# PEER encoder step on one core: w parts queued one operation later, five V buffers, two scattered tiles and three built ones

## The chip, the core and the metric

The kernel runs on one core of a Trainium2 chip. Its engines run side by side, each through its own instructions in program order: PE (TensorE, matrix products), DVE (VectorE), ACT (ScalarE), POOL (GpSimd, which also issues the indirect DMAs here) and SP (SyncE, which here only issues plain DMAs). An instruction that waits holds up everything behind it on its engine. The metric is the device time of one execution in microseconds (us), lower is better.

## The reference

The model is one layer of a streaming encoder for 1024 prompt frames and 64 sample frames of width 1024. A mixer (window attention and retention) is followed by a normalisation, then comes a feed-forward part with 16384 experts ("PEER"), which is what this change is about:

```python
s1, i1 = lax.top_k(s[:, :, 0], PEER_TOPK)          # 8 heads, 16 of 128 keys, twice
s2, i2 = lax.top_k(s[:, :, 1], PEER_TOPK)
cand_s = s1[..., :, None] + s2[..., None, :]       # 256 candidates per head
cand_i = i1[..., :, None] * N_KEYS + i2[..., None, :]
top_s, sel = lax.top_k(cand_s, PEER_TOPK)          # 16 experts per head, 128 per frame
eidx = jnp.take_along_axis(cand_i, sel, axis=-1)
g = jax.nn.softmax(top_s, axis=-1)
act = jax.nn.gelu(jnp.einsum('tpkd,td->tpk', u_tab[eidx], xb))
w = (g * act).astype(xb.dtype)
return jnp.einsum('tpk,tpkd->td', w, v_tab[eidx])
```

A frame thus has 128 pairs of an expert number and a weight g. Two heads of a frame may choose the same expert, and one head chooses 16 different ones. The output is the weighted sum of the 128 rows of `v_tab`.

## The kernel before

The 1088 frames are eight prompt tiles of 128 frames (0 to 7) and one tile TS of 64 frames. The program has three stages.

**Head.** In four groups of tiles ([TS,0,1], [2,3], [4,5], [6,7]) it computes projection, attention, retention, normalisation and the scores of the keys. A generator `route` per tile finds the 128 experts and weights. It is fed into the engines' queues in small pieces.

The feed-forward part takes two ways. For the tiles TS, 5, 6, 7 the rows of U and V are **gathered**: each of 64 + 3 x 128 = 448 slots is one indirect DMA issued by POOL (`uv`, line 239, 128 rows of 8 KB). Then DVE takes the dot product with the frame (`uv<-uv,ph`), ACT the gelu and the weight (`gav`), and DVE adds the weighted V row to `pacc`. There are four `uv` buffers (`NB`). A gather into a buffer waits for the `pacc` four slots before it.

For the tiles 0 to 4 (`DENSE`) a matrix G with a weight for each of the 16384 experts and each frame is made in HBM, and all experts are computed. G comes about in two ways:
- Tiles in `SCAT` are **scattered**: the tile's G is cleared by eight 1 MB writes of `zeros`. Then 128 indirect DMAs of POOL (line 373, `G<-sg,si`) each add one weight per frame in place. Scatters into the same G follow each other: each waits until the one before it into that G has landed. `scatter()` puts them into the program in the head, in turn over the tiles. All tiles share POOL's one queue.
- Tiles in `MIDT` are **built** in the second stage.

**Mid.** For a tile in `MIDT`, 32 steps make G from one-hot matrices. In a step DVE compares an index with a ramp (`ob`, bf16) for both halves of the expert number. POOL multiplies one by the weight (`oh<-ob,gT`) in three steps of four, and ACT turns the other to float (`oh<-ob`). In the remaining step of four DVE does it alone (`oh<-iota,gT`, four instructions, and `oh<-gT,iota`). PE multiplies them (`pG`), and ACT copies the result to `gs`. Every 16 steps 4 MB of `gs` are written to G. Beside that, mid feeds in the rest of `route` (tiles 6, 7), eight splits of the frames into a high and a low part (`xhi` on ACT, `xlo` on POOL), the first U tiles, and one scatter per step as long as some are left.

**Dense.** 128 blocks of 128 experts go through two operations. `u_mm(i)` on PE: 48 pairs of products of U's high and low parts with the frames into `pA`. Then ACT takes the gelu in place (`pA<-pA`), DVE multiplies with G (`ge<-pA,gt`), ACT makes the high part (`wh<-ge`) and POOL the low part (`wl<-ge,wh`). `v_mm` on PE: products of wh and wl with V's parts (`vh`, `vl`) for three blocks, one tile and half the width into `y`, which DVE adds to `Y`. In a group of three blocks stand three `u` operations, for the next group, and ten `v` operations. Each operation also issues the split of parts needed later: `uh` (ACT) and `ul` (POOL) of U from `ur`, `vh` (ACT) and `vl` (POOL) of V from `vr`. At each `yield` the outer loop may add up to a few gather slots. A cost model in the program, `est`, decides how many.

The order on each engine is that of the program text: whatever `u_mm` issues for ACT and POOL behind its second `yield` stands ahead of the gathers and splits that come after.

Of the kernel before, what the change touches and what calls it, by code (L numbers as in the profile page):

```python
# [9 lines left out]
F32 = mybir.dt.float32  # L10
# [5 lines left out]
OP = mybir.AluOpType  # L16
# [11 lines left out]
EPS = 1e-5  # L28
NEG = -1e30
GROUPS = [[TS, 0, 1], [2, 3], [4, 5], [6, 7]]  # L30
SCAT, MIDT = [0, 1, 2], [3, 4]
DENSE = SCAT + MIDT
ND = len(DENSE) * 128
GW = max(sum(ROWS_S if t == TS else 128 for t in g) for g in GROUPS)
# [6 lines left out]
BK = (5, 5, 5, 5, 5)  # L41
CRATE, CRMAX = 0.92, 7.0
LINK = 2.75
SCC, GTC = 1.55, 1.1
TP = 64
ATS = 4
OHB = (6, 4)
# [88 lines left out]
def hymba_peer_step(ctx, tc, a, o):  # L136
# [224 lines left out]
    def now():  # L361
        return max(est.t["pe"], est.t["dve"])
# [4 lines left out]
    def scatter(rush=0):  # L367
        n = 0
        for t in sorted(SCAT, key=lambda t: links[t]):
            if t in sc and links[t] < 128 and (n < rush or (due[t] <= now() and ctl["pq"] <= now() + 5.0)):  # L370
                g, idx = sc[t]
                j = links[t]
                nc0.gpsimd.indirect_dma_start(  # L373
                    out=spill[t]["G"], out_offset=bass.IndirectOffsetOnAxis(ap=idx[:, j:j + 1], axis=0),
                    in_=g[:, j:j + 1], in_offset=None, compute_op=OP.add)
                est.t["pool"] += 1.0
                ctl["pq"] = max(ctl["pq"], now()) + SCC
                links[t] = j + 1
                due[t] = max(due[t], now() - 3 * LINK) + LINK
                n += 1  # L380
        return n
# [856 lines left out]
    def dense(hx):  # L1238
# [13 lines left out]
        def u_fill(last):  # L1252
            while un[0] < min(last + 1, 128):
                u = up.tile([128, KC, 128], F32, name="ur")
                nc.sync.dma_start(u, a["ut"][un[0]])
                uq[un[0]] = [u]
                un[0] += 1
# [12 lines left out]
        def x_load(k):  # L1270
            xr.append(up.tile([128, ND], F32, name="xr", tag="ur"))
            nc.sync.dma_start(xr[-1], h1T_d[:, k])

        def x_split(k):
            x = xr.pop(0)
            nc.scalar.activation(xhi[:, k], x, AF.Copy)
            nc.gpsimd.tensor_tensor(xlo[:, k], x, xhi[:, k].bitcast(F32), op=OP.subtract)
# [11 lines left out]
        with ExitStack() as mx:  # L1289
            for m, _ in enumerate(mid(mx)):  # L1290
                if m % 4 == 0 and 0 <= m // 4 - 1 < KC + 2:
                    k = m // 4 - 1
                    if k >= 2:
                        x_split(k - 2)
                    if k < KC:
                        x_load(k)
                if m == 48:
                    u_fill(1)
                if m == 54:
                    u_split(0)  # L1300
                if m == 57:
                    u_split(1)
                scatter(1)
        log("mid")
# [10 lines left out]
        vp = hx.enter_context(tc.tile_pool(name="vp", bufs=NVS))  # L1315
# [12 lines left out]
        def vbase(g, h):  # L1328
            return 2 * GO[g] + h * BGS[g]
# [5 lines left out]

        def v_fill(last):
            while vn[0] < min(last + 1, NV):
                v = vp.tile([128, 512], F32, name="vr", bufs=4)
                nc.sync.dma_start(v, a["vt"][vseq[vn[0]]])
                vq[vn[0]] = [v]  # L1340
                vn[0] += 1
# [10 lines left out]
        def u_mm(i):  # L1352
            uh, ul = uq.pop(i)
            G = gq[i // 2][:, :, i % 2]
            if i % 2:
                gq.pop(i // 2)
            p = pA.tile([128, 2, 512], F32, name="pA")
            n = 0
            for l, x in ((uh, xhi), (uh, xlo), (ul, xhi)):
                for k in range(KC):  # L1360
                    for f in range(2):
                        nc.tensor.matmul(p[:, f, 0:NF], l[:, k], x[:, k, f * NF:(f + 1) * NF], start=n == 0,
                                         stop=n == 3 * KC - 1)
                    n += 1
            u_upto(i + 2)
            if i < BGS[0]:
                v_upto(i + 1)
            yield
            nc.scalar.activation(p[:, :, 0:NF], p[:, :, 0:NF], AF.Gelu_apprx_tanh)
            ge = up.tile([128, ND], F32, name="ge")  # L1370
            nc.vector.tensor_tensor(ge.rearrange("p (f n t) -> p f n t", f=2, t=TP),
                                    p[:, :, 0:NF].rearrange("p f (n t) -> p f n t", t=TP),
                                    G.rearrange("p (f n) t -> p f n t", f=2), op=OP.mult)
            whi = wp.tile([128, ND], F32R, name="wh")
            wlo = wp.tile([128, ND], F32R, name="wl")
            nc.scalar.activation(whi, ge, AF.Copy)
            nc.gpsimd.tensor_tensor(wlo, ge, whi.bitcast(F32), op=OP.subtract)
            wq[i] = (whi, wlo)
# [4 lines left out]
        def v_mm(g, h, t):  # L1383
# [11 lines left out]
            else:  # L1395
                v_upto(vbase(g, 1) + 1 + zs.index((h, t)))
            yield
            dst = Y[:, t, h * 512:(h + 1) * 512]
            if g == 0:
                nc.vector.scalar_tensor_tensor(dst, dst, ALPHA, p, op0=OP.mult, op1=OP.add)  # L1400
# [22 lines left out]
        for g in range(NG):  # L1423
            v = [("v", (g, h, t)) for h in range(2) for t in range(NT)]
# [171 lines left out]
```

## Time and profile before

| | |
|---|---|
| time, median of 3 runs | 3572.55 us (3553.33 to 3574.36) |
| profiled execution: its time, its span | 3574.14 us, 3572.4 us |
| busy in the span: PE, DVE, POOL, ACT | 81%, 64%, 55%, 30% |
| head | 0 to about 1022 us |
| mid | about 1022 to 1362 us |
| dense | 1362 us to the end |

The stage bounds are read from the instructions: the first `ob` of mid starts at 1022.44 us, the last `gs` ends at 1362.1 us. Busy time is the time in which an engine executes something. An engine can be busy half of the time and still be the one that all others wait for, if what it does stands in the wrong order. So beside the busy time the waits are read: for every engine, what ended its idle time.

### The profile page before, as it was taken

How to read it: one execution, taken by the hardware profiler on the slowest of the kernel's cores; microseconds unless marked ns; L12 is line 12 of the kernel's file. 1: busy time of each engine (PE TensorE's matmuls, PEld its weight loads, DVE VectorE, ACT ScalarE, POOL GpSimd, SP SyncE). 2: the span in 40 equal slices, each digit the busy share in tenths (PEclk: the TensorE clock that was granted, in tenths of full speed). 3: DMA queues.
4: the chain of work that ended last, by engine and by line, in shares of the span. 5: the costliest groups of instructions: out<-in, count | busy, mean ns of one | idle time of the engine just before them, and what ended most of it. 6: DMA issues, size and time to landing. Idle time of an engine off the chain costs nothing.

```text
span 3572.4 us, 43054 instructions
## 1 busy us (share of the span) xinstructions
PE 2882.9 (81%) x14953; PEld 2472.0 (69%) x14953; DVE 2273.7 (64%) x5456; ACT 1069.5 (30%) x2542; POOL 1966.4 (55%) x1430
## 2 busy tenths in 40 slices
PE   5999888998930555988888888888888888888896
PEld 3776676776720445877777777777777777778785
DVE  1438849667340992477777777777777767767734
ACT  2322332423300452232323232333233323322322
POOL 0000365665676986566565665566656655656544
PEclk8999999998965667999999999999999999999998
DMA  6337435454421356588888888888889988888841
GB/s 191 113 108 259 137 85 137 109 130 92 87 27 0 62 115 186 172 326 337 310 328 315 339 317 332 338 322 321 329 343 344 344 310 331 321 314 324 341 140 65
DMA packets 305762, 812.82 MB, mean 228 GB/s; under 512 B 80264, under 2 KB 169720, under 8 KB 238472
## 3 DMA queue, kind: packets, MB, share of 16 engines
q0 software_dynamic: 119808, 470.01, 38.4%
q1 hardware_dynamic: 185304, 339.73, 27.7%
q8 instruction: 118, 1.93, 0.2%
q14 instruction: 100, 0.82, 0.1%
q10 hardware_dynamic: 432, 0.33, 0.0%
HBM read 752.84 MB, written 56.84 MB: 227 GB/s over the span
## 4 chain that ended last, share of the span: by engine, by line
DMA 14%; issue 14%; PE 13%; POOL 11%; DVE 7%; ACT 2%; SPq 0%; POOLq 0%; DVEq 0%; ACTq 0%
DMA uv<-uv,gi 12%; PE y L108 7%; PE pA L108 6%; DVE pacc L108 4%; POOL uv L239 4%; POOL vl L108 4%; POOL ul L108 1%; POOL wl L108 1%; DVE uv L108 1%; DVE Y L108 1%; DVE ge L108 1%; ACT wh L108 1%; DMA gt<-G 1%; DMA ur<-ut 1%; POOL Y L108 0%
## 5 line engine op out<-in xcount | busy, mean ns | idle before, releaser
L373 POOL DMA_INDIRECT G<-sg,si x384 | 607.7, 1583 | 696.7 <-DMA G<-zeros 382.6
L108 DVE SCALAR_TENSOR_TENSOR uv<-uv,ph 128x1024 f32<-128x1024 f32 x448 | 544.2, 1215 | 296.8 <-DMA uv<-uv,gi 288.4
L108 PE MATMUL y<-vh,wh 128*128 128x512 f32 x1280 | 534.1, 417 | 241.2 <-DVE Y L108 223.5
L108 DVE SCALAR_TENSOR_TENSOR pacc<-uv,gav,pacc 128x1024 f32<-128x1024 f32 x448 | 575.4, 1284 | 24.0 <-ACT gav L108 21.0
L239 POOL DMA_INDIRECT uv<-uv,gi x448 | 432.3, 965 | 286.6 <-DVE pacc L108 213.6
L108 PE MATMUL y<-vl,wh 128*128 128x512 f32 x1280 | 525.8, 411 | 19.0 <-POOL vl L108 19.0
L108 PE MATMUL y<-vh,wl 128*128 128x512 f32 x1280 | 523.9, 409 | 0.0
L108 POOL TENSOR_TENSOR wl<-ge,wh 128x640 fp32r<-128x640 f32 x128 | 200.3, 1565 | 562.2 <-ACT wh L108 507.0
L108 PEld LDWEIGHTS y<-vh,wh 128*128 128x128 f32 x1280 | 253.3, 198 | 327.8 <-DVE Y L108 207.8
L108 DVE TENSOR_TENSOR Y<-y,Y 128x512 f32<-128x512 f32 x420 | 280.4, 684 | 179.9 <-PE y L108 174.8
L108 PE MATMUL pA<-xhi,uh 128*128 128x320 f32 x2048 | 337.9, 319 | 33.7 <-DVE ge L108 33.7
L108 PEld LDWEIGHTS pA<-xhi,uh 128*128 128x128 f32 x2048 | 330.6, 199 | 47.5 <-DVE ge L108 34.5
L108 POOL TENSOR_TENSOR vl<-vr,vh 128x512 fp32r<-128x512 f32 x256 | 326.1, 1292 | 11.6 <-ACT vh L108 8.7
L108 PE MATMUL pA<-xhi,ul 128*128 128x320 f32 x2048 | 321.2, 309 | 0.0
L108 PE MATMUL pA<-xlo,uh 128*128 128x320 f32 x2048 | 321.2, 309 | 0.0
L108 POOL TENSOR_TENSOR ul<-ur,uh 128x1024 fp32r<-128x1024 f32 x128 | 308.3, 2408 | 11.5 <-ACT uh L108 5.6
L108 PEld LDWEIGHTS pA<-xlo,uh 128*128 128x128 f32 x2048 | 306.0, 188 | 0.0
L108 PEld LDWEIGHTS pA<-xhi,ul 128*128 128x128 f32 x2048 | 305.6, 188 | 0.0
L108 PEld LDWEIGHTS y<-vl,wh 128*128 128x128 f32 x1280 | 254.9, 199 | 71.7 <-POOL vl L108 25.4
L108 PE MATMUL pG<-oh 128*128 128x128 f32 x512 | 109.2, 394 | 233.9 <-POOL oh L108 147.4
L108 PEld LDWEIGHTS y<-vh,wl 128*128 128x128 f32 x1280 | 254.4, 199 | 56.9
L108 ACT ACTIVATE gav<-gav 128x1 f32<-128x1 f32 x448 | 87.6, 196 | 652.0 <-DVE uv L108 617.4
(287 smaller groups left out, 4128.9 us busy)
## 6 DMA issues: line engine op xcount, KB each, us to landing
ur<-ut SPq DMA_DIRECT2D x128, 512.0 KB
vr<-vt SPq DMA_DIRECT2D x256, 256.0 KB
gt<-G SPq DMA_DIRECT2D x320, 128.0 KB
w<-w_r SPq DMA_DIRECT2D x32, 1024.0 KB
G<-zeros SPq DMA_DIRECT2D x24, 1024.0 KB
w<-w_out SPq DMA_DIRECT2D x16, 1024.0 KB
w<-w_pq SPq DMA_DIRECT2D x16, 1024.0 KB
G<-gs SPq DMA_DIRECT2D x16, 1024.0 KB
```

Source lines behind the costliest of these rows:

```text
L108: return f(*a, **k)
L239: nc0.gpsimd.indirect_dma_start(out=R, out_offset=None, in_=a["uv"], in_offset=bass.IndirectOffsetOnAxis(ap=tl[t]["idx"][:, j:j + 1], axis=0))
L373: nc0.gpsimd.indirect_dma_start(out=spill[t]["G"], out_offset=bass.IndirectOffsetOnAxis(ap=idx[:, j:j + 1], axis=0), in_=g[:, j:j + 1], in ...
```

## The change

Four edits:
- `SCAT` has two tiles instead of three, `MIDT` three instead of two: tile 2 is built. The numbers of the steps at which mid starts on U move with that (48, 54, 57 to 64, 76, 80). `SCC` is a figure of the cost model.
- The first 16 scatters of a tile (the first head, 16 different experts) write instead of adding.
- `vr` has five buffers instead of four.
- `wh` and `wl` are no longer issued in the `u_mm` that made `ge`, but by `w_split` behind the first `yield` of the operation that follows.

```diff
--- before.py
+++ after.py
@@ -28,7 +28,7 @@
 EPS = 1e-5
 NEG = -1e30
 GROUPS = [[TS, 0, 1], [2, 3], [4, 5], [6, 7]]
-SCAT, MIDT = [0, 1, 2], [3, 4]
+SCAT, MIDT = [0, 1], [2, 3, 4]
 DENSE = SCAT + MIDT
 ND = len(DENSE) * 128
 GW = max(sum(ROWS_S if t == TS else 128 for t in g) for g in GROUPS)
@@ -41,7 +41,7 @@
 BK = (5, 5, 5, 5, 5)
 CRATE, CRMAX = 0.92, 7.0
 LINK = 2.75
-SCC, GTC = 1.55, 1.1
+SCC, GTC = 1.6, 1.1
 TP = 64
 ATS = 4
 OHB = (6, 4)
@@ -372,7 +372,7 @@
                 j = links[t]
                 nc0.gpsimd.indirect_dma_start(
                     out=spill[t]["G"], out_offset=bass.IndirectOffsetOnAxis(ap=idx[:, j:j + 1], axis=0),
-                    in_=g[:, j:j + 1], in_offset=None, compute_op=OP.add)
+                    in_=g[:, j:j + 1], in_offset=None, **(dict(compute_op=OP.add) if j >= 16 else {}))
                 est.t["pool"] += 1.0
                 ctl["pq"] = max(ctl["pq"], now()) + SCC
                 links[t] = j + 1
@@ -1294,11 +1294,11 @@
                         x_split(k - 2)
                     if k < KC:
                         x_load(k)
-                if m == 48:
+                if m == 64:
                     u_fill(1)
-                if m == 54:
+                if m == 76:
                     u_split(0)
-                if m == 57:
+                if m == 80:
                     u_split(1)
                 scatter(1)
         log("mid")
@@ -1335,7 +1335,7 @@
 
         def v_fill(last):
             while vn[0] < min(last + 1, NV):
-                v = vp.tile([128, 512], F32, name="vr", bufs=4)
+                v = vp.tile([128, 512], F32, name="vr", bufs=5)
                 nc.sync.dma_start(v, a["vt"][vseq[vn[0]]])
                 vq[vn[0]] = [v]
                 vn[0] += 1
@@ -1366,11 +1366,20 @@
             if i < BGS[0]:
                 v_upto(i + 1)
             yield
+            w_split()
             nc.scalar.activation(p[:, :, 0:NF], p[:, :, 0:NF], AF.Gelu_apprx_tanh)
             ge = up.tile([128, ND], F32, name="ge")
             nc.vector.tensor_tensor(ge.rearrange("p (f n t) -> p f n t", f=2, t=TP),
                                     p[:, :, 0:NF].rearrange("p f (n t) -> p f n t", t=TP),
                                     G.rearrange("p (f n) t -> p f n t", f=2), op=OP.mult)
+            pend.append((i, ge))
+
+        pend = []
+
+        def w_split():
+            if not pend:
+                return
+            i, ge = pend.pop(0)
             whi = wp.tile([128, ND], F32R, name="wh")
             wlo = wp.tile([128, ND], F32R, name="wl")
             nc.scalar.activation(whi, ge, AF.Copy)
@@ -1395,6 +1404,7 @@
             else:
                 v_upto(vbase(g, 1) + 1 + zs.index((h, t)))
             yield
+            w_split()
             dst = Y[:, t, h * 512:(h + 1) * 512]
             if g == 0:
                 nc.vector.scalar_tensor_tensor(dst, dst, ALPHA, p, op0=OP.mult, op1=OP.add)
```

The instructions move as follows. First POOL at the border of head and mid. In the rows `G` is a tile's matrix with its number in the program (74 is tile 0, 76 tile 1, 78 tile 2), and `oh` the first products of mid. Before:

```order
L373 DMA G_76<-sg_3160,si_3162 2097152x1
L373 DMA G_78<-sg_4617,si_4619 2097152x1
L373 DMA G_74<-sg_2728,si_2730 2097152x1
L108 ISA
L108 TENSOR_TENSOR oh<-ob,gT 128x512 x5
L373 DMA G_76<-sg_3160,si_3162 2097152x1
L108 TENSOR_TENSOR oh<-ob,gT 128x512
L373 DMA G_78<-sg_4617,si_4619 2097152x1
L373 DMA G_74<-sg_2728,si_2730 2097152x1
L108 TENSOR_TENSOR oh<-ob,gT 128x512
```

The same place in the changed kernel:

```order
L373 DMA G_74<-sg_2724,si_2726 2097152x1
L373 DMA G_76<-sg_3154,si_3156 2097152x1
L373 DMA G_74<-sg_2724,si_2726 2097152x1
L373 DMA G_76<-sg_3154,si_3156 2097152x1
L108 ISA
L108 TENSOR_TENSOR oh<-ob,gT 128x512 x14
L108 TENSOR_TENSOR xlo<-xr,xhi 128x640
L108 TENSOR_TENSOR oh<-ob,gT 128x512 x3
```

Before, 310 of 384 scatters stand ahead of the first `oh` and 74 behind it. Now all 256 stand ahead of it, and none is left in mid.

Then POOL in the middle of dense, a stretch of two and a half `u` operations (`uv` a gather, `ul`, `vl`, `wl` the low parts of U, V and w). Before:

```order
L108 TENSOR_TENSOR ul<-ur,uh 128x1024
L239 DMA uv<-uv,gi 128x2048 x2
L108 TENSOR_TENSOR wl<-ge,wh 128x640
L239 DMA uv<-uv,gi 128x2048
L108 TENSOR_TENSOR vl<-vr,vh 128x512 x3
L239 DMA uv<-uv,gi 128x2048 x2
L108 TENSOR_TENSOR ul<-ur,uh 128x1024
L239 DMA uv<-uv,gi 128x2048
L108 TENSOR_TENSOR wl<-ge,wh 128x640
```

In the changed kernel:

```order
L108 TENSOR_TENSOR ul<-ur,uh 128x1024
L239 DMA uv<-uv,gi 128x2048 x2
L108 TENSOR_TENSOR wl<-ge,wh 128x640
L239 DMA uv<-uv,gi 128x2048
L108 TENSOR_TENSOR vl<-vr,vh 128x512 x2
L108 TENSOR_TENSOR ul<-ur,uh 128x1024
L239 DMA uv<-uv,gi 128x2048 x3
L108 TENSOR_TENSOR vl<-vr,vh 128x512
L108 TENSOR_TENSOR wl<-ge,wh 128x640
```

Behind `ul` one gather (`uv`) more stands ahead of `wl` than before, in two `u` of three together with a `vl`.

Last ACT at the same place (`pA<-pA` is the gelu, `vh`, `uh` and `wh` are high parts, `gav` belongs to a gather slot). Before:

```order
L108 ACTIVATE pA<-pA 128x2x320
L108 ACTIVATE wh<-ge 128x640
L108 ACTIVATE vh<-vr 128x512 x3
L108 ACTIVATE gav<-gav 128x1
L108 ACTIVATE gav<-gav,gg 128x1
```

In the changed kernel:

```order
L108 ACTIVATE pA<-pA 128x2x320
L108 ACTIVATE vh<-vr 128x512
L108 ACTIVATE gav<-gav 128x1
L108 ACTIVATE gav<-gav,gg 128x1
L108 ACTIVATE wh<-ge 128x640
L108 ACTIVATE vh<-vr 128x512 x2
```

Between the gelu and `wh` there now stand a `vh`, a slot's `gav`, or both. `wh` needs DVE's `ge`, which needs the gelu.

## Rows read from the trace of the kernel before

**Rows 1.** The page, part 1: busy us (share of the span) x instructions

```profile
PE 2882.9 (81%) x14953; PEld 2472.0 (69%) x14953; DVE 2273.7 (64%) x5456; ACT 1069.5 (30%) x2542; POOL 1966.4 (55%) x1430
```

**Rows 2.** Stretches: from:to, length, each engine's busy us (x instructions), clock, DMA, GB/s

```profile
1022.00:1163.00 141.00, 0.00 (x0) 0.00 (x0) 3.46 (x12) 2.00 (x3) 101.47 (x66) 0.50 0.19 0
1163.00:1362.00 199.00, 110.61 (x524) 101.30 (x525) 185.42 (x404) 101.83 (x131) 176.96 (x121) 0.64 0.41 83
1362.00:1398.00 36.00, 6.01 (x41) 5.74 (x40) 0.61 (x1) 2.69 (x4) 20.89 (x14) 0.62 0.76 184
```

**Rows 3.** POOL from 1160 us: start, us, engine, line, operation, count, idle before

```profile
1162.10 1.55 POOL L373 DMA_INDIRECT G<-sg,si  x1 [0.30 <-issue]
1163.19 3.62 POOL L108 TENSOR_TENSOR oh<-ob,gT 128x512 f32<-128x512 bf16 x3
```

**Rows 4.** Stretches, scatters alone: length, POOL busy us (x scatters), clock, DMA, GB/s

```profile
383.00:439.00 56.00, 22.07 (x14) 0.94 0.41 112
439.00:669.00 230.00, 132.50 (x86) 0.93 0.46 113
669.00:1022.00 353.00, 229.13 (x147) 0.95 0.44 99
1022.00:1163.10 141.10, 101.57 (x66) 0.50 0.19 0
```

**Rows 5.** Groups of instructions from 1000 to 1440 us: busy us, mean ns, idle before

```profile
L108 DVE TENSOR_TENSOR ob<-iob,ib 128x512 bf16<-128x512 bf16 x96 | 72.8, 799 | 139.4 <-POOL oh L108 139.3
L108 DVE TENSOR_SCALAR oh<-iota,gT 128x128 f32<-128x128 f32 x64 | 32.4, 575 | 0.0
L108 DVE TENSOR_TENSOR oh<-gT,iota 128x512 f32<-128x512 f32 x16 | 10.9, 679 | 0.0
...
L108 POOL TENSOR_TENSOR oh<-ob,gT 128x512 f32<-128x512 bf16 x48 | 76.1, 1612 | 6.2 <-DVE ob L108 6.1
...
L108 ACT ACTIVATE gs<-pG 128x512 f32<-128x512 f32 x64 | 66.4, 1051 | 143.3 <-PE pG L108 143.3
L108 ACT ACTIVATE oh<-ob 128x512 f32<-128x512 bf16 x48 | 31.8, 663 | 96.5 <-DVE ob L108 96.5
...
L108 PE MATMUL pG<-oh 128*128 128x128 f32 x512 | 109.2, 394 | 233.9 <-POOL oh L108 147.4 <-ACT oh L108 74.4 <-DVE oh L108 7.0
```

**Rows 6.** The instructions that use ob: count, duration in ns shortest/median/longest

```profile
L108 DVE TENSOR_TENSOR ob<-iob,ib x96: 407/413/3780, 1022.4 to 1355.0; 128x512 bf16<-128x512 bf16 x96
```

**Rows 7.** SP's queue at the end of mid: start, us, what it issued

```profile
1362.12 10.26 SPq L85 DMA_DIRECT2D G<-gs  x4
```

**Rows 8.** The chain that ended last, from mid to dense: start, us, what

```profile
1386.87 3.18 DMA G<-sg,si
...
1393.28 4.08 DMA gt<-G
1397.39 0.83 DVE ge L108
```

**Rows 9.** Waits from 1500 to 3450 us: engine, for whom, us, times, longest

```profile
POOL wl L108 <- ACT wh L108: 424.9, 100, 10.7
...
DVE uv L108 <- DMA uv<-uv,gi: 288.4, 188, 5.7
...
PE y L108 <- DVE Y L108: 223.5, 82, 8.0
...
ACT uh L108 <- DMA ur<-ut: 69.2, 29, 5.2
```

**Rows 10.** POOL around one wl of dense: start, us, operation, idle before

```profile
2402.78 0.96 POOL L239 DMA_INDIRECT uv<-uv,gi  x1 [0.16 <-issue]
2408.28 1.57 POOL L108 TENSOR_TENSOR wl<-ge,wh 128x640 fp32r<-128x640 f32 x1 [4.54 <-ACT wh L108]
2410.01 0.96 POOL L239 DMA_INDIRECT uv<-uv,gi  x1
```

**Rows 11.** DVE around the same wl: start, us, operation, idle before

```profile
2404.52 1.28 DVE L108 SCALAR_TENSOR_TENSOR pacc<-uv,gav,pacc 128x1024 f32<-128x1024 f32 x1
...
2418.35 1.22 DVE L108 SCALAR_TENSOR_TENSOR uv<-uv,ph 128x1024 f32<-128x1024 f32 x1 [2.81 <-DMA uv<-uv,gi]
```

**Rows 12.** Stretches of dense, columns as in rows 2

```profile
1966.00:2014.00 48.00, 43.23 (x232) 38.27 (x231) 35.55 (x47) 13.21 (x33) 28.46 (x23) 0.96 0.95 362
...
2000.00:2200.00 200.00, 171.49 (x913) 152.50 (x912) 147.25 (x194) 59.97 (x150) 121.94 (x95) 0.93 0.88 329
```

## The prediction

> **What bounds the kernel now.** I read the busy times first, then the stretches, the waits, and last single rows. No engine fills the span: PE is busy 81% of it, DVE 64%, POOL 55% [rows 1]. So the question is where PE stands still, and the answer differs by stage.
>
> At the start of mid everything but POOL is idle: from 1022 to 1163 us PE executes nothing, DVE 12 instructions, POOL 66 [rows 2]. Those are scatters, up to the one at 1162.10, and the first `oh` comes right behind it at 1163.19 [rows 3]. `oh` stands behind 310 scatters in one queue. DVE waits 139.3 us for it, PE 147.4 us [rows 5]. The rest of mid, from 1163 to 1362, is bound by DVE: busy 185 of 199 us, with PE at 111, ACT at 102. POOL is close with 177 [rows 2].
>
> In dense PE is busy 171.5 of 200 us, and its largest wait, 223.5 us, is for DVE's `Y` [rows 12, 9]. DVE itself waits 288.4 us for gathers in 188 waits [rows 9]; as its queue is in order, `Y` stands behind them. Gathers are late in part because POOL waits: 424.9 us in 100 waits for `wh`, with gathers queued behind [rows 9]. One case shows it. POOL issues a gather at 2402.78 and then stands 4.54 us until `wl` can start at 2408.28. The next gather goes out at 2410.01 [rows 10], though its buffer was free when `pacc` ended at 2404.52 + 1.28 = 2405.8. DVE waits 2.81 us for that gather at 2418.35 [rows 11].
>
> **Step 1, the scatters.** The first 14 go into tile 0 alone until 439 us, then 86 more alternate over tiles 0 and 1 until 669. From there tile 2 takes part, and 147 take 353 us [rows 4]. The changed kernel has the same first 100 at the same places, since its queue starts with the same tiles, and 256 - 100 = 156 are left. With two tiles instead of three a scatter has less time until its predecessor in the same G must have landed. The nearest rows give three paces: 230/86 = 2.67 us (two tiles, head running), 353/147 = 2.40 (three tiles, head running), 141.1/66 = 2.14 (three tiles, DMA quiet) [rows 4]. I take the middle one, since the last part of the 156 runs towards a quieter DMA: 669 + 156 x 2.40 = 1043 us. The bounds are 669 + 156 x 2.14 = 1003, which mid can't use before 1022, and 669 + 156 x 2.67 = 1086. The 32 plain writes and the 8 MB of zeros less lie in this queue and this stretch. No row shows an indirect write of this kind. Bounds are nothing at all, and at best the whole share of waiting in the first 14 (56 - 22 = 34 us [rows 4]), which would put the end at 1009. I take nothing. So the first `oh` moves from 1163 to 1043: **-120 us**.
>
> **Step 2, a third tile in mid.** 32 steps more. Per step, from the groups with 64 steps [rows 5]: DVE (72.8 + 32.4 + 10.9)/64 = 1.81 us, PE 109.2/64 = 1.71, ACT (66.4 + 31.8)/64 = 1.53, POOL 76.1/64 = 1.19. DVE is the largest, so 32 x 1.81 = **+58 us**. The 4 MB per 16 steps are hidden: mid moves 83 GB/s at a DMA share of 0.41 [rows 2], and 16 steps take at least 29 us. Bounds: ACT's 1.53, which gives +49 us, and the whole of the present pace with `route` and scatters in it, 199/64 = 3.11, which gives +100. DVE's `ob` says why its figure is itself uncertain: median 413 ns, longest 3780 ns [rows 6], mean 799 [rows 5], so nearly half of its time is standstill inside the instruction while POOL runs.
>
> The Trainium skill, page SBUF — State Buffer, section "Who interferes with whom", states that a DVE instruction with two SBUF inputs and a GpSimd instruction that reads SBUF exclude each other for the whole instruction. By that rule alone a step would cost the undisturbed DVE time plus the POOL time, (96 x 0.413 + 32.4 + 10.9)/64 + 1.19 = 2.49 us, and the third tile 80 us instead of 58. The long `ob` agree with the rule, while the sum of 1.81 shows that it costs less than all of POOL's time.
>
> The scatters that leave mid free POOL, but DVE binds there and its figures hold nothing of theirs that I can separate. I take no gain; the most is POOL's surplus. Mid ends at 1043 + 199 + 58 = 1300 us instead of 1362: **-62 us** for steps 1 and 2 together.
>
> **Step 3, into dense.** Now the first `gt` waits for the last scatter, which lands at 1386.87 + 3.18 = 1390 [rows 8]. Without it the last `gs` is next: issued from 1362.12 [rows 7], 4 MB at the 184 GB/s of that stretch [rows 2], landing 23 us later at 1385. **-5 us**, between 0 and the 7 us from 1390 to `ge`. PE's break of some 30 us there stays.
>
> **Step 4, `wh` and `wl` one operation later.** No instruction more, none less. The gather behind `wl` now goes out ahead of it. 100 waits of POOL each delay about one gather by 424.9/100 = 4.2 us. Of the 448 gathers 188 are waited for, 288.4/188 = 1.53 us each [rows 9]. Taking the delayed ones as average, 100 x 188/448 x 1.53 = **-64 us**, all of it ahead of a `Y` that PE waits for. What is late next: two `u` of three have a `vl` ahead of `wl`, whose `vh` stands behind the gelu on ACT, so POOL still stops there, but with one gather more on its way. `wl` itself still has three `v` operations and a `u` until PE needs it. Bounds: nothing, if DMA is already full, and 150 us, two thirds of PE's 223.5.
>
> **Step 5, the fifth `vr`.** SP's queue waits less for `vl`, so U's loads come earlier. ACT waits 69.2 us for `ur` [rows 9], hidden behind PE in most cases. Nothing; at most part of the 150.
>
> The sum: 3572.4 - 62 - 5 - 64 = 3441, and 1.7 us lie outside the span (3574.1 - 3572.4), so **3443 us**. The profiled execution is 1.6 us above the median of the runs, which needs no correction.
>
> **Rivals.**
> A. Dense gains nothing, because the bottleneck only changes its name: POOL's stop moves from `wl` to `vl`, or DMA is full. For it: DMA is busy 0.88 at 329 GB/s over 200 us [rows 12]. Against it: a stretch of 48 us reached 0.95 and 362 GB/s, and the gather in [rows 10] had a free buffer for 4.2 us. Time 3443 + 64 = 3507. The Trainium skill, page SBUF — State Buffer, section "A bandwidth-pool intuition that's wrong (but worth ruling out)", gives about 358 GB/s between HBM and one core; the estimate from it leaves 9% above 329 GB/s, and the trace's 362 agrees with the figure.
> B. Dense gains the full 150 us, since gathers that come earlier also bring the next ones earlier, and U's loads stop holding ACT: 3443 + 64 - 150 = 3357. Against it: a DMA share of 0.88 [rows 12] leaves an eighth of the time at most.
> C. Steps 1 and 2 at their bad ends, 1086 + 199 + 100 = 1385 instead of 1362: 3572.4 + 23 - 5 - 64 + 1.7 = 3528.
> D. Slower: two tiles in turn can't hide the landing, and each scatter costs what the first 14 into one tile cost, 56/14 = 4.0 us [rows 4]. Then they end at 669 + 156 x 4.0 = 1293, mid at 1550, and the time is 3443 + 250 = 3693. It decides from 669 + 156 p + 257 = 1362 + 69, that is p = 3.24 us per scatter. Against it: 2.67 us with two tiles [rows 4].
>
> **How the numbers follow.** My forecast 0.56, A 0.18, B 0.12, C 0.09, D 0.05. The predicted time is that of the first, 3443, with 3400 to 3480 as its own range. The range to give runs from just above B's time to about C's, 3360 to 3525: it leaves out D, most of B and half of C. About 1% (36 us) is what a measurement of this kernel can tell from no change, so faster means under 3537: forecast, A, B, and a third of C, whose 3528 lies close to the limit, 0.89; within 1% the rest of C, 0.06; slower D, 0.05.
>
> **What would show it.** In the new profile PE's standstill at the start of mid should be under 70 us instead of 141, with the last scatter at 1003 to 1086. Mid should run 240 to 300 us from its first `oh`, DVE busy over nine tenths. POOL's wait for `wh` should fall from 425 us to under 100, and a new wait of `vl` for `vh` should appear. DVE's wait for gathers should be 200 to 240 us, PE's wait for `Y` about 160. If DVE's wait for gathers stays near 288 with a DMA share above 0.92, A holds. If scatters go on past 1150, D does.

## The result and the profile after

The changed kernel takes 3334.4 us (median of 4 runs, 3326.08 to 3355.53) against 3572.94: a ratio of 0.9351, 95% interval 0.9305 to 0.9398, so it is faster by 239 us. The prediction was 3443 us with a range of 3360 to 3525. The direction was right. The gain is nearly twice the forecast, and the time lies below the range.

The profiled execution after took 3355.53 us (span 3353.8), the longest of the four. Where dense is read, a profile of the same kernel from e9_after_again (below), with a span of 3330.5 us, stands beside it. The page of after, part 1, answers [rows 1]:

```profile
PE 2904.7 (87%) x15212; PEld 2495.5 (74%) x15212; DVE 2265.5 (68%) x5539; ACT 1115.8 (33%) x2599; POOL 1781.7 (53%) x1326
```

PE does little more work (22 us, the third tile) in a shorter span. The time came out of standstill. Where it came from, by stage (us; the last `gs` by its end):

| | before | predicted | after | e9 |
|---|---|---|---|---|
| first `oh` of mid | 1163.2 | 1043 | 1030.2 | 1029.4 |
| last `gs`, end of mid | 1362 | 1300 | 1237.1 | 1235.4 |
| first `ge` of dense | 1397.4 | 1330 | 1261.7 | 1260.6 |
| first `ge` to the end | 2175 | 2111 | 2092 | 2070 |

Of the 242 us between the spans of before and e9, 137 stand ahead of the first `ge` (predicted 67) and 105 behind it (predicted 64). Both halves were too small.

The scatters first. Stretches of after, scatters alone, columns as in [rows 4]:

```profile
383.00:439.00 56.00, 19.77 (x20) 0.94 0.27 89
439.00:669.00 230.00, 136.85 (x93) 0.90 0.44 110
669.00:1001.50 332.50, 224.28 (x145) 0.95 0.45 102
```

By 669 us some 112 scatters are placed, not 100, and the rest go at 332.5/145 = 2.29 us each. POOL of after at the border of head and mid, as in [rows 3]:

```profile
1001.35 1.55 POOL L373 DMA_INDIRECT G<-sg,si  x1 [0.30 <-issue]
1030.22 1.15 POOL L108 TENSOR_TENSOR oh<-ob,gT 128x512 f32<-128x512 bf16 x1 [27.32 <-DVE ob L108]
```

The wait has turned round. In [rows 5] DVE waited 139.3 us for POOL's `oh`; now POOL waits 27 us for DVE's `ob`. Stretches of after, columns as in [rows 2], show why: up to 1030 us DVE is busy all the time with the rest of the head.

```profile
1002.00:1030.00 28.00, 17.02 (x99) 13.28 (x97) 27.90 (x187) 2.30 (x6) 0.91 (x1) 0.81 0.15 42
1030.00:1236.00 206.00, 132.80 (x778) 121.48 (x779) 192.75 (x502) 146.01 (x192) 118.57 (x82) 0.79 0.44 122
1236.00:1272.00 36.00, 16.15 (x92) 15.89 (x91) 0.82 (x1) 5.84 (x8) 4.26 (x5) 0.67 0.88 249
```

Mid itself takes 207 us for 96 steps, from the first `oh` to the end of the last `gs`, where 64 steps took 199. DVE is the bound as before, 94% busy. Groups of after from 1000 to 1300 us, as in [rows 5]:

```profile
L108 POOL TENSOR_TENSOR oh<-ob,gT 128x512 f32<-128x512 bf16 x72 | 99.3, 1386 | 108.3 <-DVE ob L108 105.5 <-PE pG L108 2.9
L108 DVE TENSOR_TENSOR ob<-iob,ib 128x512 bf16<-128x512 bf16 x144 | 74.0, 559 | 3.4 <-POOL oh L108 3.3
L108 DVE TENSOR_SCALAR oh<-iota,gT 128x128 f32<-128x128 f32 x96 | 48.5, 566 | 0.4 <-PE pG L108 0.4
```

144 `ob` now take 74.0 us where 96 took 72.8: the mean fell from 799 to 559 ns. POOL, whose queue no longer holds scatters, waits 105 us for DVE, not 6.

In dense the waits from the first `ge` to the end (before from 1397 us, columns as in [rows 9]) were:

```profile
POOL wl L108 <- ACT wh L108: 507.0, 112, 11.7
...
DVE uv L108 <- DMA uv<-uv,gi: 288.4, 188, 5.7
...
PE y L108 <- DVE Y L108: 223.5, 82, 8.0
POOL uv L239 <- DVE pacc L108: 213.6, 122, 7.6
```

The same of after, from 1261 us:

```profile
POOL uv L239 <- DVE pacc L108: 561.2, 266, 8.0
...
DVE uv L108 <- DMA uv<-uv,gi: 234.0, 112, 5.2
PE y L108 <- DVE Y L108: 182.9, 87, 8.7
...
POOL wl L108 <- ACT wh L108: 86.3, 42, 12.0
POOL vl L108 <- ACT vh L108: 49.9, 14, 8.0
```

POOL's stop at `wl` fell from 507 to 86 us and DVE's wait for gathers from 288 to 234 us, as step 4 said, and a small new wait of `vl` for `vh` appeared. PE's wait for `Y` fell by 41 us only (by 47 in e9, to 176.6), not by 64. POOL's largest wait is now for `pacc`, that is, for a free gather buffer. And yet dense lost 83 us here and 105 in e9, about twice what PE lost in waits for `Y`. The experiments show why.

### The profile page after: what moved, and what is told of

Its sections match the earlier page's. It is cut to its first block, busy times and chain, and to the rows that moved or that the text cites. A ratio compares the mean times of both kernels' runs of the same rounds, so it can differ in the third digit from the quotient of the medians.

```text
span 3353.8 us, 43782 instructions
## 1 busy us (share of the span) xinstructions
PE 2904.7 (87%) x15212; PEld 2495.5 (74%) x15212; DVE 2265.5 (68%) x5539; ACT 1115.8 (33%) x2599; POOL 1781.7 (53%) x1326
## 4 chain that ended last, share of the span: by engine, by line
PE 39%; DVE 22%; DMA 13%; issue 11%; POOL 10%; ACT 3%; SPq 1%; POOLq 0%; DVEq 0%; ACTq 0%
PE pA L108 13%; PE y L108 10%; DMA uv<-uv,gi 9%; PE pv L108 4%; PE pq L108 4%; DVE VI L108 4%; PE pa L108 3%; POOL uv L239 3%; POOL vl L108 3%; DVE pacc L108 3%; DVE ge L108 2%; DVE ob L108 2%; POOL ul L108 2%; POOL wl L108 2%; DVE oh L108 2%
## 5 line engine op out<-in xcount | busy, mean ns | idle before, releaser
L373 POOL DMA_INDIRECT G<-sg,si x256 | 382.3, 1493 | 620.2 <-DVE si L108 383.3
L108 ACT ACTIVATE pA<-pA 128x640 f32<-128x640 f32 x128 | 88.0, 688 | 511.9 <-PE pA L108 505.9
L108 DVE TENSOR_TENSOR ge<-pA,gt 128x640 f32<-128x640 f32 x128 | 105.2, 822 | 212.0 <-ACT pA L108 145.3
```

Of the source, the lines that this page charges most:

```text
L108: return f(*a, **k)
L373: nc0.gpsimd.indirect_dma_start(out=spill[t]["G"], out_offset=bass.IndirectOffsetOnAxis(ap=idx[:, j:j + 1], axis=0), in_=g[:, j:j + 1], in ...
```

## The experiments

Each run stands against the kernel before, run beside it. "Gather stretch" is the time from the first to the last product of DVE with a gathered row, read from the instructions; 448 gathers lie in it.

### The change in two halves

e1_defer_alone is the kernel before with `w_split` alone (step 4); e2_tiles_alone is the kernel before with the tiles and step numbers alone (steps 1 to 3, no plain writes, no fifth `vr`); e3_no_defer is the changed kernel without `w_split`.

In e3 both calls of `w_split` go, and in `u_mm` stands again:

```diff
-            pend.append((i, ge))
+            whi = wp.tile([128, ND], F32R, name="wh")
+            wlo = wp.tile([128, ND], F32R, name="wl")
+            nc.scalar.activation(whi, ge, AF.Copy)
+            nc.gpsimd.tensor_tensor(wlo, ge, whi.bitcast(F32), op=OP.subtract)
+            wq[i] = (whi, wlo)
```

> The kernel before with the later wh and wl alone. Theory P (step 4 of the prediction was about right, the miss lies in mid): 64 to 75 us less than before, so about 3500 us; POOL's wait for wh under 100 us, mid unchanged with its 141 us standstill. Rival Q (the miss lies in dense: the later wh and wl gained the 171 us that steps 1 to 3 leave of the 238): about 3400 us.

> The kernel before with two scattered and three built tiles alone (all scatters add, vr has four buffers, wh and wl at their old place). Theory P: mid ends near 1240 us instead of 1362, and the time is 3573 - 125 - 11 = about 3437 us. Rival Q: steps 1 to 3 were right, 67 us less, about 3506 us.

> The changed kernel with wh and wl back in the operation that makes ge. Theory P: 64 to 75 us above the changed kernel's 3334, about 3404 us. Rival Q: about 3500 us.

Measured: e1 3445.04 us (ratio 0.964, 0.96 to 0.9679), 124 us under before. e2 3463.58 us (0.9702, 0.9662 to 0.9741), 105 us under it. e3 3489.83 us (0.9758, 0.9717 to 0.9799), 155 us over the changed kernel. The halves add up: 124 + 105 = 229 of 239 us. Neither theory holds: each had all of the miss in one half, and both halves were too small. Step 4 is worth 124 us alone and 155 us taken out of the whole, not 64. In e2 the first `ge` comes 140 us earlier, but dense grows by 26 us to 2201. Its gathers start 35 us behind the first `ge` instead of 91, and so 52 us more of dense lie behind the last of them. These two nearly cancel. What is left is that the 448 gathers themselves take 1955 us instead of 1926, though about as many `v` operations lie among them (375, before 374). That price stood in no step, and its cause stays open.

e3 differs from e2 by the plain writes and the fifth `vr`, and is 26 us slower. That effect isn't there once `wh` and `wl` come later (e4, e9 and e10). Its cause stays open.

The gather stretch of e1, then the same of before (columns as in [rows 2]):

```profile
1475.80:3286.70 1810.90, 1642.30 (x8804) 1462.02 (x8802) 1393.17 (x1850) 605.33 (x1470) 1160.17 (x899) 0.97 0.94 348
```

```profile
1488.00:3413.00 1925.00, 1667.73 (x8805) 1477.73 (x8804) 1403.51 (x1848) 596.69 (x1465) 1162.79 (x898) 0.95 0.87 327
```

The same work in 115 us less. Of the 130 us between the two profiled spans 12 more lie ahead of the first `ge`, where e1 changes nothing: the scatters of this execution came earlier.

### The plain writes

e4_all_add is the changed kernel in which all scatters add.

```diff
-                    in_=g[:, j:j + 1], in_offset=None, **(dict(compute_op=OP.add) if j >= 16 else {}))
+                    in_=g[:, j:j + 1], in_offset=None, compute_op=OP.add)
```

> The changed kernel with all scatters adding. Theory P: the plain writes only bring the last scatter earlier by up to 34 us, from 1003 to at most 1037, while mid starts at 1030 anyway: 3334 to 3341 us. Rival R (the plain writes are what emptied POOL's queue in time): the last scatter past 1090 us, and 3395 us or more.

Measured: 3335.94 us (0.9336, 0.9297 to 0.9375), the time of the changed kernel, as theory P said. The scatters of after and of e4 (count, duration in ns shortest/median/longest, first and last start):

```profile
L373 POOL DMA_INDIRECT G<-sg,si x256: 952/1554/1987, 383.7 to 1001.4; - x128
```

```profile
L373 POOL DMA_INDIRECT G<-sg,si x256: 1539/1548/1987, 385.2 to 1020.4; - x128
```

A plain write costs POOL from 0.95 us, one that adds 1.54. The last scatter starts 19 us later without them. But the first `ob` comes at 1020 to 1030 us in these profiles, when DVE is done with the head, so it is worth nothing, as step 1 had it.

### What mid gains when the scatters leave it

e5_hold_scatters is the changed kernel, but 37 scatters per tile are held back for mid: 74, as many as stood behind the first `oh` before.

The cap is 91 in the head and 128 from mid on.

```diff
-            if t in sc and links[t] < 128 and (n < rush or (due[t] <= now() and ctl["pq"] <= now() + 5.0)):
+            if t in sc and links[t] < ctl["cap"] and (n < rush or (due[t] <= now() and ctl["pq"] <= now() + 5.0)):
```

> The changed kernel, but only 91 scatters per tile are put into the head and the last 74 go into mid, one per step, as in the kernel before. Theory S (the scatters in POOL's queue slowed mid itself): the 96 steps take 206 + 74 x 1 us, the difference per scatter between before and after, so about 280 us, and the time is about 3400 us. Rival D (the prediction: DVE binds mid and scatters cost nothing there): 206 us and about 3334 us; the faster mid would then come from something else.

Measured: 3387.59 us (0.9484, 0.9445 to 0.9522), 53 us over the changed kernel. Theory D has fallen. Mid of e5, from the first `oh` to the last `gs`:

```profile
1022.00:1298.20 276.20, 157.78 (x786) 142.93 (x787) 226.37 (x501) 149.92 (x192) 228.50 (x156) 0.66 0.43 91
```

276 instead of 207 us: a scatter in mid costs 69/74 = 0.94 us. POOL is busy 228 us, not 119, and DVE's share falls to 0.82. Before, 62 of the 74 started in mid itself and 12 behind it: 62 x 0.94 = 58 us of its 199, if a scatter cost as much there.

e8_no_pool_mid is the changed kernel with `BTS = 1`: DVE makes the first one-hot matrix in every step, POOL none.

```diff
-BTS = 4
+BTS = 1
```

> The changed kernel with the first one-hot matrix of mid made by DVE in all steps, none by POOL (384 TENSOR_SCALAR instead of 96, 72 ob fewer). Theory L (in mid DVE loses time standing while POOL computes): undisturbed rows near 0.28 us for TENSOR_SCALAR and 0.36 for ob give 384 x 0.28 + 72 x 0.36 + 24 x 0.6 = 148 us, and 45 for route: mid under 200 us, time 3325 to 3334 us. Rival O (DVE's long rows are its own cost, 0.57 us per TENSOR_SCALAR): mid about 300 us, time about 3430 us.

Measured: 3334.51 us (0.9332, 0.929 to 0.9374). Rival O has fallen; theory L had mid a little too short. Mid of e8, and groups of DVE in it:

```profile
1028.40:1235.00 206.60, 138.88 (x775) 124.11 (x775) 196.57 (x715) 144.69 (x191) 18.20 (x10) 0.77 0.44 122
```

```profile
L108 DVE TENSOR_SCALAR oh<-iota,gT 128x128 f32<-128x128 f32 x376 | 115.9, 368 | 0.0
L108 DVE TENSOR_TENSOR ob<-iob,ib 128x512 bf16<-128x512 bf16 x71 | 29.3, 413 | 0.0
L108 DVE TENSOR_TENSOR oh<-gT,iota 128x512 f32<-128x512 f32 x24 | 16.3, 679 | 0.0
...
L108 DVE TENSOR_TENSOR ge<-ge,lanes 128x1024 bf16<-128x1024 bf16 x4 | 2.7, 681 | 0.0
```

DVE takes over all of POOL's `oh` and mid still lasts 208 us from the first `ob` to the last `gs` (207 in after). With POOL out of it, DVE's instructions get shorter: `oh<-iota,gT` 368 ns against 566 in after, `ob` 413 against 559, and `ge<-ge,lanes`, an instruction of `route`, 681. The same instruction takes in mid of before, then of after:

```profile
L108 DVE TENSOR_TENSOR ge<-ge,lanes 128x1024 bf16<-128x1024 bf16 x4 | 5.7, 1432 | 0.0
```

```profile
L108 DVE TENSOR_TENSOR ge<-ge,lanes 128x1024 bf16<-128x1024 bf16 x4 | 4.4, 1106 | 0.0
```

These means mix two cases. One by one, the four instructions take 0.68, 0.68, 1.52 and 2.84 us in before, 1.53, 0.68, 0.68 and 1.53 in after, and 0.68 each in e8. An instruction of DVE isn't slowed all along here: it takes its own time or it is held. `ob` shows the same: in after 122 of 144 take 0.40 to 0.43 us, as all do in e8, 18 take about 1.26, 4 about 1.78, and none lies between. With scatters and `oh` on POOL the mean of the four is 1432 ns, with `oh` alone 1106, without 681. What POOL's `oh` spare DVE in work, they cost it in standstill. How a scatter's part in this comes about no run separates.

### wl alone

e6_wl_alone is the changed kernel with `wh` at its old place on ACT; only `wl` on POOL comes one operation later.

```diff
+            whi = wp.tile([128, ND], F32R, name="wh")
+            nc.scalar.activation(whi, ge, AF.Copy)
-            pend.append((i, ge))
+            pend.append((i, ge, whi))
```

> The changed kernel with wh back at its old place on ACT, and only wl on POOL one operation later. Theory W (all of the gain of the later parts is POOL's: gathers no longer stand behind wl): 3330 to 3345 us, time from buffer free to gather issue about 0.8 us. Rival A (a part of it is ACT's: gav, vh and uh no longer stand behind wh, which waits for ge): 3365 to 3400 us.

Measured: 3380.54 us (0.9452, 0.941 to 0.9494), as rival A said: 109 of the 155 us come from `wl` on POOL, 46 from `wh` on ACT. Waits of e6, 1500 to 3130 us:

```profile
ACT wh L108 <- DVE ge L108: 215.0, 98, 6.9
...
PE y L108 <- DVE Y L108: 184.9, 82, 10.3
...
POOL vl L108 <- ACT vh L108: 52.7, 34, 4.3
```

ACT stands at `wh` for `ge`, with `vh` and the slots' gelu behind it. POOL's `vl` waits for that `vh` (52.7 us, 4.7 in after over the same time), and gathers stand behind `vl`.

### The number of V buffers

e7_vr4 is the changed kernel with four `vr` buffers; e9_after_again and e10_vr4_again repeat the two side by side.

```diff
-                v = vp.tile([128, 512], F32, name="vr", bufs=5)
+                v = vp.tile([128, 512], F32, name="vr", bufs=4)
```

> The changed kernel with four vr buffers. Theory C (the fifth buffer lets SP send loads earlier, into the gathers, and costs what the two kernels without the later parts differ by, 26 us): about 3308 us, ACT's wait for ur near 70 us again. Rival N (the fifth buffer does nothing or helps; those two kernels differ by something else): 3334 us or more.

> The changed kernel once more, so that the number of V buffers (four against five) and the spread of the gathers are compared in runs taken side by side. Both theories: 3334 us (3326 to 3340).

> The changed kernel with four V buffers instead of five, again. Theory N (the fifth buffer does nothing once the parts of w come later, as step 5 said): within 0.2% of the changed kernel, 3328 to 3341 us. Theory X (it costs, because SP's queue no longer stands at vl, U's loads of 512 KB go out earlier and meet the gathers): 3322 to 3328 us, at least 6 us under the changed kernel in the same comparison, so that the first comparison's 7.5 us repeat. Without the later parts of w the fifth buffer went with 26 us more (3464 to 3490).

Measured: e7 3326.88 us (0.9306, 0.9268 to 0.9344), e9 3329.11 us (0.9306, 0.9288 to 0.9325), e10 3324.95 us (0.9303, 0.9283 to 0.9323). The fifth buffer does nothing to the time that can be measured, so theories C and X have fallen. It does end ACT's wait for `ur` (101 us in e7 and 90 in e10, under 2 in after and e9), which thus was hidden, as step 5 said.

### What sets the time of dense

In e9 the gathers end 210 us before the kernel does. Its gather stretch and what follows:

```profile
1297.00:3120.00 1823.00, 1644.23 (x8794) 1463.84 (x8793) 1390.92 (x1847) 599.75 (x1465) 1160.87 (x898) 0.96 0.92 346
3120.00:3330.00 210.00, 177.27 (x966) 159.26 (x965) 66.34 (x97) 47.36 (x69) 99.33 (x72) 0.93 0.25 81
```

e11_spread spreads them to the end by one figure of the program's cost model. The instructions are the same; the last gather slot stands behind 422 of dense's 430 `v` operations instead of 378. e12_spread_vr4 is the same with four `vr`.

```diff
-        est.t["dma"] = max(est.t["dma"], max(est.t["pe"], est.t["dve"]) - 3.0) + 2.6
+        est.t["dma"] = max(est.t["dma"], max(est.t["pe"], est.t["dve"]) - 3.0) + 2.9
```

> The changed kernel with the gathers spread to the end of dense: the cost model's pace 2.9 us per gather instead of 2.6, so the last of the 448 slots stands at operation 422 of 430 of the last group and not about 210 us before the end. Same instructions. Theory B (while gathers run the DMA is the bound, at a share of 0.92 and 342 GB/s; the 210 us behind the last gather leave it idle): a gather stretch of some 2020 us at a share of 0.85, waits of PE for Y and of DVE for gathers at half, time 3270 to 3310 us. Theory L (PE's own work binds with gathers or without, and what is saved per gather is lost by more operations that hold one): 3325 to 3345 us, as before. Theory O (the order gets worse: the last gathers' results come late at the end): over 3345 us.

> Spread gathers and four V buffers together. Theory B with X: the lower of the two single results, less about 7 us more. Theory L with N: 3325 to 3345 us. It is the version that could beat the changed kernel if both single edits gain.

Measured: e11 3198.73 us (0.8948, 0.8924 to 0.8971), e12 3203.86 us (0.8946, 0.8925 to 0.8967). That is 130 us under the changed kernel, more than any theory allowed, and the fastest version here. Its stretches:

```profile
1288.00:3152.00 1864.00, 1772.74 (x9721) 1585.12 (x9720) 1431.74 (x1905) 634.53 (x1525) 1241.33 (x947) 0.99 0.93 346
3152.00:3197.00 45.00, 11.65 (x42) 8.78 (x42) 25.93 (x40) 7.62 (x8) 23.07 (x23) 0.67 0.18 70
```

The gather stretch grew by only 41 us, although 129 us more of PE's work lie in it. So the 448 gathers took nearly the same time whatever stood beside them, and PE was not what they waited for.

Two theories were left: the DMA's rate (346 GB/s both times) or the round of the four `uv` buffers. e13_more_bytes adds a load of 256 KB, read by nobody, to every second V load (four `vr`); e14_spread_no_defer is e11 without `w_split`.

```diff
                 vq[vn[0]] = [v]
+                if vn[0] % 2 == 0:
+                    z = vp.tile([128, 512], F32, name="zr", bufs=1)
+                    nc.sync.dma_start(z, a["vt"][vseq[vn[0]]])
```

> The changed kernel with four V buffers, and in the room of the fifth a further plain load of 256 KB for every second V load (128 loads, 33.5 MB, read by nobody). It measures what bytes cost in dense. Theory B (while gathers run the DMA binds, at 346 GB/s whatever is asked of it): about nine tenths of the 33.5 MB fall beside the gathers, 30 MB at 346 GB/s are 87 us; the gather stretch goes from 1821 to 1890 to 1920 us at the same 340 to 350 GB/s, time 3325 + 70 to 100 = 3395 to 3425 us. Theory W (POOL's stops and the landing time of single gathers bind, and the DMA has room up to the 362 to 366 GB/s of single stretches): the rate rises to 355 to 362 GB/s, the stretch grows by under 40 us, time 3325 to 3365 us.

> The spread gathers with wh and wl at their old place, that is without step 4. Base 3199 us. Theory B with the closed loop (POOL's stop at wl holds the next gather and by that the rate: 318 GB/s in this arrangement with crowded gathers): 643 MB at 318 to 327 GB/s are 1966 to 2022 us instead of 1864, time 3300 to 3360 us. Theory P (once the gathers are spread there is slack for each, and PE at 95% binds): under 3250 us.

Measured: e13 3250.32 us (0.911, 0.9076 to 0.9144), e14 3371.43 us (0.9425, 0.9393 to 0.9456). Both lie outside what either of their theories gave.

e13 needs care. The cost model counts the added loads, so the program also spreads its gathers further, to operation 403. On the line between e10 (378, 3325 us) and e12 (422, 3204 us) that place alone gives 3325 - 121 x 25/44 = 3256 us. The mean distance between two gathers, 4.14 us, also lies between those of e10 (4.09) and e12 (4.20). So 33.5 MB more cost about nothing. Its gather stretch:

```profile
1289.00:3137.00 1848.00, 1721.87 (x9364) 1537.34 (x9363) 1420.32 (x1881) 625.09 (x1504) 1215.49 (x930) 0.98 0.97 364
```

364 GB/s: the rate of 346 was not a ceiling, and the theory that the DMA binds at that rate has fallen. e14 shows that step 4 is worth 173 us where the gathers are not crowded, so its size doesn't hang on crowding.

e15_nb3 takes away one `uv` buffer of e11, e16_nb5 adds one. For the room e16 has three `vr` and five `vh` and `vl` buffers; e17_nvs5 is e11 with that alone.

The edits of e15, and then those that make e16 (e17 is without the first pair):

```diff
-NB, LEAD = 4, 3
+NB, LEAD = 3, 2
```

```diff
-NB, LEAD = 4, 3
+NB, LEAD = 5, 4
-NVS, NWB = 6, 6
+NVS, NWB = 5, 6
-                v = vp.tile([128, 512], F32, name="vr", bufs=5)
+                v = vp.tile([128, 512], F32, name="vr", bufs=3)
```

> The spread version with three uv buffers for the gathers instead of four (NB, LEAD = 3, 2). Base 3199 us, 448 gathers in 1864 us, 4.16 us each, so one round of a buffer (issue, landing, DVE's two products, ACT's gelu, free again) takes 4 x 4.16 = 16.6 us. Theory R (the round of the buffers sets the pace): 14.5 to 16.6 us by three, 4.8 to 5.5 us per gather, a stretch of 2160 to 2480 us, time 3490 to 3820 us. Theory E (an engine or the rate of the DMA sets it, the buffers have slack): under 3280 us.

> The spread version with five uv buffers (NB, LEAD = 5, 4); for room three vr buffers and five of vh and vl. To be read against e17_nvs5, which has the same room taken away and four uv buffers. Theory R: the pace falls until PE binds, which is busy 1773 of 1864 us now; at 1800 us of stretch 65 us less than e17_nvs5, 30 to 80 us with what DVE still waits. Theory E: within 15 us of e17_nvs5.

> The spread version with three vr buffers instead of five and five of vh and vl instead of six, the control of e16_nb5. Both theories: 3195 to 3260 us; V's parts are made a product later at most.

Measured: e15 3590.26 us (1.0045, 1.0028 to 1.0063), e16 3235.85 us (0.9056, 0.9017 to 0.9096), e17 3286.39 us (0.9187, 0.9155 to 0.9218). One buffer fewer costs 391 us, as the theory of the round said; one more gains 50 us against e17. The missing buffers of V cost 87 us (e17 against e11), more than expected. The gather stretches of e15, e16 and e17:

```profile
1289.00:3576.00 2287.00, 1865.86 (x9759) 1655.90 (x9758) 1453.54 (x1934) 642.82 (x1530) 1258.49 (x969) 0.90 0.79 283
```

```profile
1299.00:3187.00 1888.00, 1778.53 (x9713) 1590.08 (x9712) 1425.48 (x1903) 630.11 (x1525) 1238.87 (x944) 0.98 0.92 341
```

```profile
1299.00:3241.00 1942.00, 1795.38 (x9717) 1602.29 (x9717) 1438.25 (x1904) 633.57 (x1525) 1236.28 (x945) 0.98 0.90 332
```

PE is busy 82% of the stretch with three buffers, 92% with four and 94% with five (e15, e17, e16).

Where the time of a round goes can be read from the timelines of POOL and DVE, pairing each gather in order with its product on DVE, and with the `pacc` that frees its buffer. In DVE's order `pacc` of a slot stands behind the product of the next slot. So N buffers give N - 1 paces per round: pace = (issue to product + product of the next slot to the end of `pacc` + buffer free to issue) / (N - 1). Means over some 420 gathers each, in us:

| | issue to product | to the end of `pacc` | free to issue | pace, sum/(N-1) |
|---|---|---|---|---|
| before | 8.56 | 2.49 | 1.93 | 4.33 |
| e1, `w_split` alone | 8.95 | 2.44 | 0.81 | 4.07 |
| e3, without `w_split` | 8.88 | 2.50 | 1.99 | 4.46 |
| e6, `wl` alone | 9.28 | 2.50 | 0.91 | 4.23 |
| e9, the changed kernel | 9.05 | 2.43 | 0.78 | 4.09 |
| e14, spread, without `w_split` | 9.09 | 2.51 | 2.27 | 4.62 |
| e11, spread | 9.37 | 2.42 | 0.77 | 4.19 |
| e15, three buffers | 6.91 | 2.43 | 0.98 | 5.16 |
| e17, less room for V | 9.45 | 2.77 | 0.90 | 4.37 |
| e16, e17 with five buffers | 13.33 | 2.82 | 0.88 | 4.26 |

The last column also is the distance of the gathers' issues as measured, to 0.01 us. It must be: the three parts and the pace are differences of the same instants, so the sum holds whatever sets the time. The table is a breakdown and no test. It shows where a change took time out of the round; that the round sets the pace is shown by e15. And the round does so only up to a point. From its landing to its product a gather lies 0.35 us on average in e15, 1.6 in e11 and 5.4 in e16. With three buffers a gather is used almost as soon as it lands. With five it waits for DVE's turn, so the buffers no longer set the pace alone; that a sixth would give little is argued from this and was not run.

## Why the prediction was right and wrong

**What bounds the kernel: half right.** POOL's queue at the start of mid, DVE in mid and POOL's stop at `wl` were the right places. In dense I took PE's wait for `Y` as what the time would follow. While gathers run it is mainly the round of their four buffers that sets the time (e15), and PE has room: in e11 it does 129 us more work beside the same gathers.

**Step 1, right and small.** 1043 us was forecast for the last scatter; it starts at 1001, at the edge of the lower bound of 1003, and mid starts at 1030 because DVE still works on the head. I had the same 100 scatters at 669 us as before and the pace of three tiles. 112 stand there, which explains most of it (12 x 2.4 = 29 of 42 us). The plain writes, which I put at nothing, bring most of these 12: where all add, 102 stand there and the last scatter starts at 1020 (e4). That a time before 1022 can't be used held, so they are worth nothing to the kernel.

**Step 2 failed in one term.** "The scatters that leave mid free POOL, but DVE binds there [...] I take no gain" was the step. It put at nothing what e5 measured as 62 x 0.94 = 58 us. The 58 us for the third tile were about right: 199 + 58 - 58 = 199 us, where mid took 207. The rows pointed to it: `ob` with a median of 413 and a mean of 799 ns [rows 5, 6] means some 37 us of standstill in `ob` alone. I read it as uncertainty of a price, not as a cost of which a part leaves with the scatters (the mean is 559 ns in after).

On the Trainium skill's rule (page SBUF — State Buffer, section "Who interferes with whom"), that the two engines exclude each other for a whole instruction: read one by one, the instructions of after agree. Two cases, POOL's `oh` beside the same kind of instruction of `route` on DVE:

```profile
1065.76 1.10 POOL L108 TENSOR_TENSOR oh<-ob,gT 128x512 f32<-128x512 bf16 x1 [0.89 <-DVE ob L108]
1065.88 1.53 DVE L108 TENSOR_TENSOR ge<-posf,lanes 128x1024 bf16<-128x1024 bf16 x1
...
1079.09 1.70 POOL L108 TENSOR_TENSOR oh<-ob,gT 128x512 f32<-128x512 bf16 x1 [3.95 <-DVE ob L108]
1079.20 0.68 DVE L108 TENSOR_TENSOR ge<-bpos,lanes 128x1024 bf16<-128x1024 bf16 x1
```

First DVE is held (1.53 us instead of the 0.68 of e8) while POOL takes 1.10, near its shortest `oh` of 1.03. Then POOL is held (1.70) while DVE takes 0.68. That the estimate of 2.49 us per step lies above the 207/96 = 2.16 measured doesn't speak against the rule: its 1.19 us for POOL come from `oh` of 1612 ns on average, so POOL's own standstill is counted in them.

**Step 3** was right in kind: from the last `gs` to the first `ge` 35.3 us became 24.6 us, -11 where -5 was forecast.

**Step 4, the mechanism right, the size wrong.** The failing sentence is "100 waits of POOL each delay about one gather [...] 100 x 188/448 x 1.53 = -64". It counts each delay once, and only where DVE waited for that very gather. But the buffers go round: a gather that goes out late is used late, its buffer comes free late, and so does the next gather into that buffer. So the delay counts for all gathers, divided by N - 1. By the breakdown in the table, e1 against before: 448/3 x (1.93 - 0.81) = 167 us less, given back in part since a gather now takes longer to its product, 448/3 x (8.95 - 8.56) = 58 us, and 7 us less from `pacc`: -116 us, where the stretch fell by 115. Why a gather then takes longer to its product no run separates. Of the waits that I named as signs, `wl` and `uv` came as forecast, and PE's for `Y` fell by less than forecast (41 to 47 us, not 64) while dense fell by more: what a wait of PE falls by is not what the stretch falls by.

**Step 5** held in the changed kernel (e7, e9, e10). Without `w_split` something costs 26 us between e2 and e3, which stays open.

**The rivals.** B named the right mechanism, "gathers that come earlier also bring the next ones earlier", and its 150 us are what e3 shows (155). That the time of 3334 us lies near B's 3357 is luck, though: mid gave some 70 us more than B had, dense 45 less. I gave it 0.12 because a DMA share of 0.88 seemed to leave an eighth at most. The share rose to 0.92 and the rate to 346 GB/s, and e13 reached 0.97 and 364 GB/s. Dense as a whole keeps 105 of them: with the tiles alone it is 26 us longer than before, with all but step 4 53 us (2175, 2201 in e2, 2228 in e3, 2070 in e9). A, C and D did not come. In part POOL's stop did change its name, as A has it: its wait for a free buffer grew from 214 to 561 us. The figure of about 358 GB/s (the Trainium skill, page SBUF — State Buffer, section "A bandwidth-pool intuition that's wrong (but worth ruling out)") stands beside 364 GB/s that e13 moved over 1848 us. That is a little more, and the measurement decides: 358 was no ceiling here.

## What to carry to other kernels

A stage that goes round a few buffers has its time from the round: before a delay is priced by the waits that it causes now, it is to be added to the round and divided by the buffers in turn, for every element. Here that is an upper bound: it gives 167 us for `w_split` alone, and 115 came. Instructions whose mean is far above their median are standing still in part, and look for the neighbour that holds them: some of the cost leaves with it. Where a stage runs out of its slow work before its end, spread that work: here one number in a cost model gave 130 us more, over half of what the whole change brought.

## What the runs showed that I had not expected

- A scatter of 128 elements costs mid 0.94 us, though POOL issues it and not DVE, which binds there, and though POOL's `oh` fill under half of mid (99 of 207 us).
- An indirect DMA that writes takes POOL from 0.95 us, one that adds 1.54 us.
- 33.5 MB more of plain loads beside the gathers, at 364 instead of 346 GB/s, cost no time that shows.
- With one gather fewer on its way a gather takes 6.91 us from its issue to its product instead of 9.37. Of these 2.5 us, 1.2 are a shorter way from issue to landing (6.5 instead of 7.7 us) and 1.3 a shorter wait behind it. So of a fourth buffer's share in the pace a part is lost again to longer waiting.
